# Seven-product FFN chunks that add up in PSUM, and gate chunk 2 in that form too

## The chip, the cores and the metric

The kernel runs on one core of a Trainium2 chip. The metric is the device time in microseconds of one execution; three executions are given, and one more was profiled.

## What is computed

A decoder trunk of two layers on one sequence of 512 tokens with 1024 features, in fp32. Each layer is: half a SwiGLU FFN, a mixer (gated linear attention in the first layer, stick-breaking attention in the second), half a SwiGLU FFN. So there are four FFNs, and they are where the change is:

```python
def rmsnorm(x, g):
    return x * rsqrt(mean(x * x, axis=-1) + EPS) * g

def swiglu(h, w_gate, w_up, w_down):      # D_FF = 2816
    return (silu(h @ w_gate) * (h @ w_up)) @ w_down

x = x + 0.5 * swiglu(rmsnorm(x, ffn_norm), w_gate, w_up, w_down)
```

## The kernel before

Activations lie with features on the 128 partitions and the 512 tokens along the free axis. A product that must keep fp32 accuracy is made of three matmuls on rounded operands: a value is cut in a high part (ScalarE, ACT: a cast) and a low part (VectorE, DVE: value minus high part), and high x high, low x high and high x low are added up in PSUM. Names ending in h and l are these parts (wh, wl of weights; nh, nl of the normed input; hh, hl of a result that goes into the down projection).

**The queue.** All weight work is a list of entries in `feed.q`. Each entry has units (a weight chunk and a view of it) and a body with its matmuls. `Feed.start` (called as each entry begins) first splits the weights of this entry and the next two (at most four buffers of 1024 columns, tag wh and wl), then loads the raw chunks of six entries (two raw buffers of 1 MB), then runs the body. The framework puts the instructions on the engines' queues; among those that are ready the earlier in the program goes first.

**An FFN.** The 2816 gate and up columns are 11 chunks of 256 columns, c = 0 to 10. A plain chunk is two entries of `feat`, each 24 matmuls of 512 columns (8 blocks of features in, three matmuls each) into one tile ps_f. In the order of the queue, counted from the FFN's start: e0 to e3 are gate and up of chunk 0, e4 to e7 those of chunk 1, e8 and e9 gate of chunk 2; then come the chunks of `seven` (gate from chunk 3 on by `SEVEN`, up from chunk 2 on by `SEVEN_UP`), with entries of the down projection of the group before (`down`, 24 matmuls of 512 columns) put between them.

**Seven products.** `seven` computes a chunk as a 2 x 2 block product (features in by features out, with the tokens in two halves of H = 256) with seven block products in place of eight (Winograd's form of Strassen's scheme). Each product is 12 matmuls of 256 columns (4 blocks, three matmuls each). A chunk is two entries: `body_1` has four products (P1 to P4 in the prediction), `body_2` has three (P5 to P7). `body_1` uses the view ax of the raw weights and the weight sums s12, `body_2` uses the sums s34 and the view a22. The sums (`sums_12`, `sums_34`) are four DVE operations of 512 columns into tiles of tag s, and are made when the entry is split. On the input side the products use nh, nl and the eight input sums th, tl (`t_half`): t sums 0, 2, 4, 6 in `body_1`, and 1, 3, 5, 7 in `body_2`. Before the change, P1 to P7 end in these tiles and operations: w (copied to u2 by ACT, L545), z (added to u2 by DVE), q (copied to c5 by ACT, L552), w again (then Silu or the product with the gate), z's other half (u3 = z + u2, o1 = u3 + c5, on DVE), q again (o0 = q + u2, on DVE), w's other half (o1 = w + u3, on DVE).

**Start of an FFN.** `run` lets e0 and e1 run on input that isn't normed yet, while the statistics and their row R are made (`stats_a`, `stats_b`). Before each of e2 to e5, one piece of `normed_input` runs: two blocks scaled (xn, L592), split (nh, nl), and four differences for one tile ts (L608) of tag s, so that after four pieces the four buffers of tag s hold ts. Then `sums` makes the eight input sums, each half a ts tile: a cast th on ACT and a subtraction tl on DVE (both L598 and L599), in pieces 0 to 7, two before each of e6 to e9. A buffer of tag s is free again when both halves of its ts are split, and the weight sums s12 and s34 use the same four buffers.

Of the kernel before, what the change touches and what calls it, by code (L numbers as in the profile page):

```python
# [18 lines left out]
P = 128  # L19
T = 512  # L20
# [12 lines left out]
def decoder(ctx: ExitStack, tc: tile.TileContext, a: dict, out: bass.AP):  # L33
# [13 lines left out]
    def psum(name, tag=None):  # L47
        if tag is None:
            tag = order[turn_[0] % 8]
            turn_[0] += 1  # L50
        return pp.tile([P, T], F32, tag=tag, bufs=banks[tag], name=name)
# [11 lines left out]
    def mm(ps, l, r, first, last):  # L63
        nc.tensor.matmul(ps, l, r, start=first, stop=last)  # L64
# [27 lines left out]
    class Entry:  # L92
# [3 lines left out]

        def __init__(self, units, body, place=0, lead=False):
            self.units, self.body, self.W, self.place = units, body, None, place
            self.lead = lead

        def split(self):
            if self.W is None:
                self.W = []
                for ch, view, n, m in self.units:
                    r = view(ch.load())
                    few = n * m < 1024
                    if few:

                        h = st["few"].tile([P, n * m + NEAR], F32R, tag="vh", bufs=1, name="wh")[:, NEAR:]
                        l = st["few"].tile([P, n * m + 64 - NEAR], F32R, tag="vl", bufs=1, name="wl")[:, : n * m]  # L110
                    else:
                        h, l = (
                            wp.tile([P, n * m + 64], F32R, tag="w" + t, bufs=4, name="w" + t)[
                                :, self.place : self.place + n * m
                            ]
                            for t in "hl"
                        )
                    h, l = (t.rearrange("p (n m) -> p n m", m=m) for t in (h, l))
                    st["cut"] = nc.scalar.copy(h, r).ins  # L119
                    with tc.issue_after(st["gains"]):  # L120
                        nc.vector.tensor_tensor(out=l, in0=r, in1=h.bitcast(F32), op=ALU.subtract)  # L121
                    self.W.append((h, l))
                    if self.lead and len(self.W) == 1:

                        first = wp.tile([P, m], F32R, tag="w1", bufs=1, name="w1")
                        nc.scalar.copy(first, r[:, 0])
                        self.first = first

    class Feed:
# [3 lines left out]
        def start(self):  # L133
            i = self.pos
            self.pos += 1
            used = 0
            for e in self.q[i : i + 3]:
                used += sum(n * m >= 1024 for _, _, n, m in e.units)
                if used > 4:
                    break  # L140
                e.split()
            for e in self.q[i : i + 6]:
                for u in e.units:
                    u[0].load()
            e = self.q[i]
            return e.body(e.W)
# [234 lines left out]
    def stats_b(tag=None):  # L381

        ps = psum("ps_R", tag)
        dgs = sp.tile([P, T], F32, tag="ss", name="dg")
        for i in range(NT):
            dg = dgs[:, i * P : (i + 1) * P]
            nc.vector.tensor_scalar(
                out=dg, in0=ident, scalar1=st["r4"][:, i : i + 1], scalar2=None, op0=ALU.mult
            )
            mm(ps[:, i * P : (i + 1) * P], ones, dg, True, True)  # L390
        st["R"] = sp.tile([P, T], F32, tag="sq", name="R")
        nc.vector.tensor_copy(st["R"], ps)

# [28 lines left out]
    class FFN:  # L422
# [4 lines left out]


        GROUPS = ((0, 2), (2, 4), (4, 6), (6, 8), (8, 9), (9, 11))
        NORMED, SEVEN = 6, 3  # L430
        SEVEN_UP = (2, 3, 4, 5, 6, 7, 8, 9, 10)

        def __init__(self, wg, wu, wd, gi, nxt, first=False, last=False):
# [49 lines left out]
        def seven(self, ch, group=None):  # L483
# [30 lines left out]
            def half(k0, c):  # L514
                return lambda j: (st["h"][k0 + j][:, c * H : c * H + H], st["l"][k0 + j][:, c * H : c * H + H])

            def part(name):
                return self.tp.tile([P, H], F32, tag="c", bufs=2, name=name)

            def add(o, x, y):  # L520
                nc.vector.tensor_tensor(out=o, in0=x, in1=y, op=ALU.add)

            def left(o, w):
                if group is None:
                    nc.scalar.activation(o[:, 0:H], w, AF.Silu)
                else:
                    nc.vector.tensor_tensor(out=o[:, 0:H], in0=w, in1=self.gates[0][:, 0:H], op=ALU.mult)

            def rest(o, c):
                if group is None:  # L530
                    st["silu"] = nc.scalar.activation(o[:, c:T], o[:, c:T], AF.Silu).ins
                    self.gates.append(o)
                    return
                nc.vector.tensor_tensor(out=o[:, c:T], in0=o[:, c:T], in1=self.gates.pop(0)[:, c:T], op=ALU.mult)
                self.close(o, group)

            def body_1(W):
                ax, s = W

                v["w"], v["z"], v["q"] = psum("ps_w"), psum("ps_z"), psum("ps_q")  # L540
                w, z, q = (v[n][:, 0:H] for n in "wzq")
                v["o"] = self.tp.tile([P, T], F32, tag="t", name="o0")
                prod(w, ax, 0, half(0, 0), lead=entry.first if lead else None)
                v["u2"] = part("u2")
                nc.scalar.copy(v["u2"], w)  # L545
                yield
                prod(z, s, 4, lambda j: self.t_half(1, j))
                add(v["u2"], z, v["u2"])
                yield
                prod(q, s, 0, lambda j: self.t_half(0, j))  # L550
                v["c5"] = part("c5")
                nc.scalar.copy(v["c5"], q)  # L552
                yield
                prod(w, ax, 4, half(4, 0), first=False)
                left(v["o"], w)
                yield

            def body_2(W):
                s, a22 = W
                q, y = v["q"][:, 0:H], v["z"][:, H:T]  # L560
                o0, o1 = v["o"], self.tp.tile([P, T], F32, tag="t", name="o1")
                prod(y, s, 0, lambda j: self.t_half(2, j))
                u3 = o1[:, 0:H]
                add(u3, y, v["u2"])
                nc.vector.tensor_tensor(out=o1[:, H:T], in0=u3, in1=v["c5"], op=ALU.add)
                yield
                prod(q, s, 4, half(4, 1), first=False)
                add(o0[:, H:T], q, v["u2"])
                rest(o0, H)
                yield  # L570
                o = v["w"][:, H:T]
                prod(o, a22, 0, lambda j: self.t_half(3, j))
                add(o1[:, 0:H], o, u3)
                rest(o1, 0)
                yield


# [47 lines left out]
        def sums(self):  # L625
            def piece(i):

                h = np_.tile([P, T], F32R, tag="xh", name="th")
                l = np_.tile([P, T], F32R, tag="xl", name="tl")
                self.ts[i] = self.cut(h, l, self.ts[i].rearrange("p a b -> p (a b)"))  # L630

            return [lambda i=i: piece(i) for i in range(KD)]

        def evac_g(self, ps):
            t = self.tp.tile([P, T], F32, tag="t", name="t")
# [17 lines left out]
        def run(self, between=None):  # L653
            with tc.tile_pool(name="hp", bufs=8, reuse_waits="tile") as self.hp, tc.tile_pool(
                name="tp", bufs=5, reuse_waits="tile"
            ) as self.tp:
                st["few"] = self.hp
                new_norm()
                two_halves(stats_a)
                stats_b()  # L660
                flush(self.defer)
                for job, n in ((self.normed_input, self.NORMED - 2), (self.sums, self.sums_by - self.NORMED)):
                    todo = list(job())
                    for i in range(n):
                        for piece in todo[i * len(todo) // n : (i + 1) * len(todo) // n]:
                            piece()
                        feed.entries(1)
                    self.normed = True
                    st["h"], st["l"] = zip(*self.n)
                feed.entries(self.count - self.sums_by)  # L670
                if between is not None:
                    with tc.issue_after(st["silu"]):
                        nc.scalar.preload_act_table_set("sqrt_and_others")
                    feed.q[feed.pos].split()
                    between(self.tp)
                feed.entries(self.total - self.count)
# [636 lines left out]
```

## Time and profile before

| | us |
|---|---|
| three executions | 1870.85, 1871.63, 1871.76 |
| median | 1871.63 |
| the profiled execution | 1871.49 |
| its span on the core | 1869.6 |
| TensorE (PE) busy | 1849.7 (99%) |
| DVE busy | 1456.8 (78%) |
| ACT busy | 954.0 (51%) |

Busy times are those of the profiled execution, and the shares are of its span. PE is the matmul stream and PEld its weight loads, which overlap it. In the rows of the profile, L64 are the matmuls of the plain entries and of the down entries, L510 those of the seven-product chunks, L119 and L121 the casts and subtractions that split weights, L493 to L500 the weight sums, L598 and L599 the split of inputs and results, and L297 the addition of a down product to x. The mean of a matmul in a row is longer than the distance from one to the next, since matmuls overlap; the distance is what counts.

### The profile page before, as it was taken

Reading aid. Unit: us, or ns where it says so; the run is one execution under the profiler, and the core shown is the slowest. Engines: PE = TensorE matmul, PEld = TensorE weight load, DVE = VectorE, ACT = ScalarE, POOL = GpSimd, SP = SyncE. Lnnn points to the kernel's source line nnn. Section 1 sums busy time; section 2 is a strip of 40 time slices with the busy share of each in tenths; the row PEclk is TensorE's granted clock in tenths of the full one; section 3 lists DMA queues with packets and bytes.
Section 4 is the critical chain, followed back from the end, with each engine's and each line's share of the span. In section 5 each row is a group of like instructions: output and inputs, shape, how many; then the busy total and the mean of one; then the engine's idle time right before and its main releaser. Section 6 shows DMA issues by size and latency. Waiting matters only on the chain.

```text
span 1869.6 us, 28889 instructions
## 1 busy us (share of the span) xinstructions
PE 1849.7 (99%) x11789; PEld 1647.6 (88%) x11789; DVE 1456.8 (78%) x2313; ACT 954.0 (51%) x1506; POOL 7.3 (0%) x17
## 2 busy tenths in 40 slices
PE   8999999999999999999999999999999999999998
PEld 6899999789887899999888999998888788999997
DVE  7978777775766988877888778776878769778785
ACT  6534434444555544444554444445888755444444
POOL 0000000100000000000000000000000000000000
PEclk9999999999999999999999999999999999999999
DMA  5423333212223233342233333233221223333321
GB/s 158 146 91 112 103 113 105 86 50 65 64 72 113 77 104 103 108 129 80 79 113 124 102 102 113 79 93 100 68 68 57 68 91 95 120 102 102 119 85 68
DMA packets 177514, 179.03 MB, mean 96 GB/s; under 512 B 4035, under 2 KB 167925, under 8 KB 177381
## 3 DMA queue, kind: packets, MB, share of 16 engines
q1 hardware_dynamic: 176768, 176.18, 30.1%
q8 instruction: 92, 1.51, 0.3%
q0 software_dynamic: 512, 0.99, 0.2%
q14 instruction: 42, 0.34, 0.1%
q10 hardware_dynamic: 100, 0.03, 0.0%
HBM read 175.11 MB, written 2.10 MB: 95 GB/s over the span
## 4 chain that ended last, share of the span: by engine, by line
PE 96%; DVE 2%; ACT 1%; DMA 1%; issue 0%; DVEq 0%; ACTq 0%; SPq 0%
PE ps_d L64 25%; PE ps_f L64 20%; PE ps_w L510 15%; PE ps_z L510 10%; PE ps_q L510 10%; PE ps_t L64 5%; PE ps_b L64 4%; PE ps_S L64 1%; PE ps_z L1044 1%; PE ps_bt L64 1%; PE ps_oT L1106 1%; PE ps_T L1091 1%; PE ps_o L64 1%; DVE wl L121 0%; DMA raw<-in_ffn_w_up_dram 0%; PE ps_R L64 0%
## 5 line engine op out<-in xcount | busy, mean ns | idle before, releaser
L121 DVE TENSOR_TENSOR wl<-raw,wh 128x1024 fp32r<-128x1024 f32 x244 | 261.3, 1071 | 81.8 <-ACT wh L119 71.6
L119 ACT CAST wh<-raw 128x1024 fp32r<-128x1024 f32 x244 | 226.5, 932 | 137.4 <-PE ps_f L64 44.3
L64 PE MATMUL ps_d<-hh,wl 128*128 128x512 f32 x672 | 262.1, 390 | 0.0
L64 PE MATMUL ps_d<-hh,wh 128*128 128x512 f32 x672 | 262.1, 390 | 0.0
L64 PE MATMUL ps_d<-hl,wh 128*128 128x512 f32 x672 | 261.4, 389 | 0.0
L119 ACT CAST wh<-s 128x1024 fp32r<-128x1024 f32 x136 | 142.8, 1050 | 142.4 <-PE ps_q L510 70.4
L297 DVE SCALAR_TENSOR_TENSOR x<-ps_d,x 128x512 f32<-128x512 f32 x184 | 125.6, 688 | 87.6 <-PE ps_d L64 87.4
L121 DVE TENSOR_TENSOR wl<-s,wh 128x1024 fp32r<-128x1024 f32 x136 | 166.2, 1222 | 25.9 <-ACT wh L119 15.3
L64 PE MATMUL ps_f<-xh,wh 128*128 128x512 f32 x448 | 181.7, 406 | 3.1 <-DVE q L707 1.5
L64 PE MATMUL ps_f<-xl,wh 128*128 128x512 f32 x448 | 175.0, 391 | 0.0
L64 PE MATMUL ps_f<-xh,wl 128*128 128x512 f32 x448 | 174.5, 389 | 0.0
L119 ACT CAST wh<-rawd 128x1024 fp32r<-128x1024 f32 x84 | 88.5, 1054 | 150.7 <-PE ps_d L64 127.6
L510 PE MATMUL ps_z<-th,wh 128*128 128x256 f32 x544 | 150.3, 276 | 0.0
L510 PE MATMUL ps_z<-th,wl 128*128 128x256 f32 x544 | 150.2, 276 | 0.0
L510 PE MATMUL ps_z<-tl,wh 128*128 128x256 f32 x544 | 150.1, 276 | 0.0
L510 PE MATMUL ps_w<-nh,wl 128*128 128x256 f32 x544 | 150.1, 276 | 0.0
L510 PE MATMUL ps_w<-nl,wh 128*128 128x256 f32 x544 | 150.1, 276 | 0.0
L64 PEld LDWEIGHTS ps_d<-hl,wh 128*128 128x128 f32 x672 | 126.2, 188 | 26.7
L64 PEld LDWEIGHTS ps_d<-hh,wh 128*128 128x128 f32 x672 | 126.2, 188 | 24.8
L64 PEld LDWEIGHTS ps_d<-hh,wl 128*128 128x128 f32 x672 | 126.1, 188 | 24.1
L121 DVE TENSOR_TENSOR wl<-rawd,wh 128x1024 fp32r<-128x1024 f32 x84 | 102.9, 1225 | 42.8 <-ACT wh L119 33.6
L510 PE MATMUL ps_w<-nh,wh 128*128 128x256 f32 x488 | 134.7, 276 | 0.0
(249 smaller groups left out, 4711.7 us busy)
## 6 DMA issues: line engine op xcount, KB each, us to landing
raw<-in_ffn_w_gate_dram SPq DMA_DIRECT2D x43, 1024.0 KB, 5.4
raw<-in_ffn_w_up_dram SPq DMA_DIRECT2D x43, 1024.0 KB, 5.3
rawd<-in_ffn_w_down_dram SPq DMA_DIRECT2D x84, 512.0 KB, 3.5
raw<-in_gla_w_in_dram SPq DMA_DIRECT2D x12, 1024.0 KB, 5.3
raw<-in_sb_w_in_dram SPq DMA_DIRECT2D x16, 512.0 KB, 3.8
raw<-in_gla_w_out_dram SPq DMA_DIRECT2D x4, 1024.0 KB, 5.1
raw<-in_sb_w_in_dram SPq DMA_DIRECT2D x4, 1024.0 KB, 5.1
raw<-in_sb_w_out_dram SPq DMA_DIRECT2D x4, 1024.0 KB, 5.0
```

The costliest lines, as they stand in the source:

```text
L64: nc.tensor.matmul(ps, l, r, start=first, stop=last)
L119: st["cut"] = nc.scalar.copy(h, r).ins
L121: nc.vector.tensor_tensor(out=l, in0=r, in1=h.bitcast(F32), op=ALU.subtract)
L297: nc.vector.scalar_tensor_tensor(out=xs[k], in0=ps, scalar=0.5, in1=xs[k], op0=ALU.mult, op1=ALU.add)
L510: nc.tensor.matmul(o, l_, r_, start=first and j + n == 0, stop=j == 3 and n == 2, skip_group_check=True)
L1044: nc.tensor.matmul(o_, l_, r_, start=first, stop=last, skip_group_check=True)
L1091: nc.tensor.transpose(ps[:, c0 : c0 + P], ys[yb][:, yc + j * P : yc + (j + 1) * P], ident)
L1106: nc.tensor.matmul(po[e * 64 : e * 64 + 64, j * P : T], self.v[j][:, c : c + 64], self.wt[p, e][bk][:, c0 : c0 + n], start=j == 0, stop=j ...
```

## The change

It has five parts. (1) `SEVEN` is 2 in place of 3, so that the gate columns of chunk 2 are also made in seven products: e8 and e9 are then `body_1` and `body_2` of that chunk, and one down entry follows each chunk of this group. (2) In the bodies, three products go on adding in w (P1, P3, P5, P7, with copies of the sums in between), and z begins as an ACT copy of w after P1, onto which P4 adds. ACT copies q into o1, w into o0 and w into u3. Three DVE additions and the tiles u2 and c5 go. The Silu, or the product with the gate, is made in four parts of 256 columns by `gate`. (3) `Feed.start` also makes the views, and so the weight sums, of one entry more than it splits (`view`). (4) The input sums are made in the order 0, 1, 2, 4, 6, then `body_1` of the first seven-product chunk, then 3, 5, 7; the first five stand before e6 and e7. (5) The four matmuls of `stats_b` that spread R are one accumulation group of the bank.

```diff
         def split(self):
-                for ch, view, n, m in self.units:
-                    r = view(ch.load())
+                for r, (_, _, n, m) in zip(self.view(), self.units):
...
                 e.split()
+            for e in self.q[i : i + 4]:
+                e.view()
...
-            mm(ps[:, i * P : (i + 1) * P], ones, dg, True, True)
+            nc.tensor.matmul(
+                ps[:, i * P : (i + 1) * P], ones, dg, start=i == 0, stop=i == NT - 1, skip_group_check=True
+            )
...
-        NORMED, SEVEN = 6, 3
+        NORMED, SEVEN = 6, 2
...
+            def gate(o, c, t):
+                if group is None:
+                    st["silu"] = nc.scalar.activation(o[:, c : c + H], t, AF.Silu).ins
                 else:
+                    g = self.gates[0 if o is v["o"][0] else 1]
+                    nc.vector.tensor_tensor(out=o[:, c : c + H], in0=t, in1=g[:, c : c + H], op=ALU.mult)
             def body_1(W):
                 ax, s = W
...
                 prod(w, ax, 0, half(0, 0), lead=entry.first if lead else None)
-                v["u2"] = part("u2")
-                nc.scalar.copy(v["u2"], w)
-                yield
-                prod(z, s, 4, lambda j: self.t_half(1, j))
-                add(v["u2"], z, v["u2"])
+                nc.scalar.copy(z, w)
                 yield
                 prod(q, s, 0, lambda j: self.t_half(0, j))
-                v["c5"] = part("c5")
-                nc.scalar.copy(v["c5"], q)
-                yield
-                prod(w, ax, 4, half(4, 0), first=False)
-                left(v["o"], w)
+                nc.scalar.copy(o1[:, H:T], q)
+                yield
+                prod(w, s, 4, lambda j: self.t_half(1, j), first=False)
+                nc.scalar.copy(o0[:, H:T], w)
+                yield
+                prod(z, ax, 4, half(4, 0), first=False)
+                gate(o0, 0, z)
                 yield
             def body_2(W):
                 s, a22 = W
...
-                prod(y, s, 0, lambda j: self.t_half(2, j))
-                u3 = o1[:, 0:H]
-                add(u3, y, v["u2"])
-                nc.vector.tensor_tensor(out=o1[:, H:T], in0=u3, in1=v["c5"], op=ALU.add)
+                prod(w, s, 0, lambda j: self.t_half(2, j), first=False)
+                u3 = self.tp.tile([P, H], F32, tag="c", bufs=1, name="u3")
+                nc.scalar.copy(u3, w)
+                nc.vector.tensor_tensor(out=o1[:, H:T], in0=u3, in1=o1[:, H:T], op=ALU.add)
                 yield
                 prod(q, s, 4, half(4, 1), first=False)
-                add(o0[:, H:T], q, v["u2"])
-                rest(o0, H)
-                yield
-                o = v["w"][:, H:T]
-                prod(o, a22, 0, lambda j: self.t_half(3, j))
-                add(o1[:, 0:H], o, u3)
-                rest(o1, 0)
+                nc.vector.tensor_tensor(out=o0[:, H:T], in0=q, in1=o0[:, H:T], op=ALU.add)
+                gate(o0, H, o0[:, H:T])
+                if group is not None:
+                    self.close(o0, group)
+                gate(o1, H, o1[:, H:T])
+                yield
+                prod(w, a22, 0, lambda j: self.t_half(3, j), first=False)
+                gate(o1, 0, w)
...
-            return [lambda i=i: piece(i) for i in range(KD)]
+            return [lambda i=i: piece(i) for i in (0, 1, 2, 4, 6, 3, 5, 7)]
...
-                for job, n in ((self.normed_input, self.NORMED - 2), (self.sums, self.sums_by - self.NORMED)):
...
+                spread(self.normed_input(), self.NORMED - 2)
+                self.normed = True
+                st["h"], st["l"] = zip(*self.n)
+                todo = self.sums()
+                spread(todo[:5], self.sums_by - self.NORMED)
+                feed.entries(1)
+                for piece in todo[5:]:
+                    piece()
+                feed.entries(self.count - self.sums_by - 1)
```

More of the change, by code (lines that the diff above doesn't have):

```diff
@@ L98, in __init__, with view @@
             self.units, self.body, self.W, self.place = units, body, None, place
-            self.lead = lead
+            self.lead, self.views = lead, None
+        def view(self):
+            if self.views is None:
+                self.views = [view(ch.load()) for ch, view, _, _ in self.units]
+            return self.views
         def split(self):
@@ L515, in half @@
                 return lambda j: (st["h"][k0 + j][:, c * H : c * H + H], st["l"][k0 + j][:, c * H : c * H + H])
[L517 to L523, printed above, removed]
+            def gate(o, c, t):
                 if group is None:
-                    nc.scalar.activation(o[:, 0:H], w, AF.Silu)
+                    st["silu"] = nc.scalar.activation(o[:, c : c + H], t, AF.Silu).ins
@@ L526, in left @@
                 else:
[L527 to L535, printed above, removed]
+                    g = self.gates[0 if o is v["o"][0] else 1]
@@ L537, in body_1 @@
+                    nc.vector.tensor_tensor(out=o[:, c : c + H], in0=t, in1=g[:, c : c + H], op=ALU.mult)
             def body_1(W):
                 ax, s = W
-                v["w"], v["z"], v["q"] = psum("ps_w"), psum("ps_z"), psum("ps_q")
-                w, z, q = (v[n][:, 0:H] for n in "wzq")
-                v["o"] = self.tp.tile([P, T], F32, tag="t", name="o0")
+                v["w"], v["q"] = psum("ps_w"), psum("ps_q")
+                z = psum("ps_z")[:, 0:H]
+                w, q = (v[n][:, 0:H] for n in "wq")
@@ L543, in body_1 @@
+                o0, o1 = v["o"] = [self.tp.tile([P, T], F32, tag="t", name=n) for n in ("o0", "o1")]
                 prod(w, ax, 0, half(0, 0), lead=entry.first if lead else None)
-                v["u2"] = part("u2")
-                nc.scalar.copy(v["u2"], w)
-                yield
-                prod(z, s, 4, lambda j: self.t_half(1, j))
-                add(v["u2"], z, v["u2"])
+                nc.scalar.copy(z, w)
                 yield
                 prod(q, s, 0, lambda j: self.t_half(0, j))
-                v["c5"] = part("c5")
@@ L559, in body_2 @@
                 s, a22 = W
-                q, y = v["q"][:, 0:H], v["z"][:, H:T]
-                o0, o1 = v["o"], self.tp.tile([P, T], F32, tag="t", name="o1")
-                prod(y, s, 0, lambda j: self.t_half(2, j))
-                u3 = o1[:, 0:H]
-                add(u3, y, v["u2"])
-                nc.vector.tensor_tensor(out=o1[:, H:T], in0=u3, in1=v["c5"], op=ALU.add)
+                w, q = (v[n][:, 0:H] for n in "wq")
+                o0, o1 = v["o"]
+                prod(w, s, 0, lambda j: self.t_half(2, j), first=False)
+                u3 = self.tp.tile([P, H], F32, tag="c", bufs=1, name="u3")
+                nc.scalar.copy(u3, w)
+                nc.vector.tensor_tensor(out=o1[:, H:T], in0=u3, in1=o1[:, H:T], op=ALU.add)
                 yield
                 prod(q, s, 4, half(4, 1), first=False)
-                add(o0[:, H:T], q, v["u2"])
-                rest(o0, H)
-                yield
-                o = v["w"][:, H:T]
-                prod(o, a22, 0, lambda j: self.t_half(3, j))
-                add(o1[:, 0:H], o, u3)
-                rest(o1, 0)
+                nc.vector.tensor_tensor(out=o0[:, H:T], in0=q, in1=o0[:, H:T], op=ALU.add)
[3 more added lines that the diff above has]
+                gate(o1, H, o1[:, H:T])
+                yield
+                prod(w, a22, 0, lambda j: self.t_half(3, j), first=False)
+                gate(o1, 0, w)
+                if group is not None:
+                    self.close(o1, group)
+                    del self.gates[:2]
+                else:
+                    self.gates += [o0, o1]
                 yield
@@ L661, in run, with spread @@
                 flush(self.defer)
-                for job, n in ((self.normed_input, self.NORMED - 2), (self.sums, self.sums_by - self.NORMED)):
-                    todo = list(job())
+                def spread(todo, n):
                     for i in range(n):
@@ L667, in run @@
                         feed.entries(1)
-                    self.normed = True
-                    st["h"], st["l"] = zip(*self.n)
-                feed.entries(self.count - self.sums_by)
+                spread(self.normed_input(), self.NORMED - 2)
[7 more added lines that the diff above has]
+                feed.entries(self.count - self.sums_by - 1)
                 if between is not None:
```

## The prediction

> **What bounds the kernel now.** I read the page first (shares, then the chain that ended last), then the chain in order of time, then the busy time by stretch of the first feed-forward stage, then the queues of VectorE (DVE) and ScalarE (ACT) there.
>
> ```profile
> span 1869.6 us, 28889 instructions
> PE 1849.7 (99%) x11789; PEld 1647.6 (88%) x11789; DVE 1456.8 (78%) x2313; ACT 954.0 (51%) x1506; POOL 7.3 (0%) x17
> PE 96%; DVE 2%; ACT 1%; DMA 1%; issue 0%; DVEq 0%; ACTq 0%; SPq 0%
> ```
>
> TensorE (PE) carries 96% of the chain. The chain by pieces shows how tightly: start, length, engine and tile.
>
> ```profile
> 27.75 43.56 PE ps_f L64 x192
> 610.60 43.56 PE ps_f L64 x192
> 948.95 43.56 PE ps_f L64 x192
> 1532.80 43.56 PE ps_f L64 x192
> ...
> 71.31 1.36 PE ps_w L510 x12
> ...
> 124.40 1.36 PE ps_q L510 x12
> ...
> 127.12 1.36 PE ps_z L510 x12
> ```
>
> The four FFN stages open alike: eight plain entries (e2 to e9) of 24 matmuls of 512 columns each, 192 in 43.56 us, so 226.9 ns a matmul and 5.445 us an entry, without a gap; then seven-product chunks, 12 matmuls of 256 columns in 1.36 us, 113.3 ns each. So a product P1 to P7 is 1.36 us. PE has no slack to give back here except fewer matmul columns.
>
> The second fact is DVE. Columns: stretch, its length, then busy time (and count) of PE, PEld, DVE, ACT, POOL, granted clock, DMA share, GB/s.
>
> ```profile
> 28.00:49.00 21.00, 21.00 (x94) 17.33 (x94) 21.00 (x39) 13.61 (x20) 0.00 (x0) 1.00 0.04 10
> 49.00:71.00 22.00, 22.00 (x99) 18.22 (x98) 21.95 (x34) 10.53 (x16) 0.00 (x0) 1.00 0.48 151
> 71.00:90.00 19.00, 19.00 (x169) 18.96 (x168) 16.21 (x26) 11.22 (x17) 0.00 (x0) 1.00 0.43 137
> ...
> 120.00:353.00 233.00, 233.00 (x1616) 215.64 (x1615) 185.21 (x279) 106.29 (x161) 2.43 (x3) 1.00 0.33 105
> ```
>
> From 28 to 71 us DVE is busy 42.95 of 43 us; later it is at 79% (185.21 of 233). At the opening two engines are full at once, and the chunk that changes its form lies exactly there.
>
> **Part 1: gate chunk 2 in seven products.** It removes e8 and e9 (48 matmuls x 226.9 ns = 10.89 us) and adds 84 matmuls x 113.3 ns = 9.52 us. Gain 1.37 us per FFN, 5.5 us for four, as long as PE stays without gaps. The Trainium skill (TensorE: Matmul & The Clock Gate, "Wait — 56ns, not 53.3ns?") adds a fixed 2.5 ns per matmul to N divided by 2.4 GHz, which speaks against halving the columns; by it 48 x 215.8 − 84 x 109.2 gives 1.19 us, an estimate, 4.7 us in all. The rows show no such term (113.3 is half of 226.9), so 5.5 stands. The granted clock is 1.00 in every stretch above and nothing here lowers it.
>
> **Part 2: the bodies of the 68 (now 72) chunks.** Three DVE additions of 256 columns go (u2, u3, the last o1), two ACT copies come, and a 512-column product or Silu becomes two of 256.
>
> ```profile
> L521 DVE TENSOR_TENSOR u<-ps_z,u 128x256 f32<-128x256 f32 x68 | 28.6, 420 | 12.5 <-PE ps_z L510 12.5
> L545 ACT COPY u<-ps_w 128x256 f32<-128x256 f32 x68 | 25.3, 372 | 10.7 <-PE ps_w L510 7.6
> ```
>
> DVE loses about 3 x 0.42 us of busy time a chunk, ACT gains 2 x 0.37. Neither is on the chain in the steady part, so it is worth nothing there by itself. What is new is what PE waits for: P3 (into w) for the copy z<-w, P5 (into w) for o0<-w, P7 for u3<-w. Each copy has one product, 1.36 us, to get done. The steady part shows ACT at these points:
>
> ```profile
> 121.76 1.06 ACT L119 CAST wh<-rawd 128x1024 fp32r<-128x1024 f32 x1 [1.64 <-PE ps_d L64]
> 122.72 0.29 ACT L126 CAST w<-raw 128x128 fp32r<-128x128 f32 x1
> 123.08 0.37 ACT L545 COPY u<-ps_w 128x256 f32<-128x256 f32 x1
> 125.86 0.37 ACT L552 COPY c<-ps_q 128x256 f32<-128x256 f32 x1 [2.40 <-PE ps_q L510]
> 126.12 1.05 ACT L119 CAST wh<-raw 128x1024 fp32r<-128x1024 f32 x1
> ```
>
> The third product ends at 125.76 (124.40 + 1.36), the copy then runs to 126.23, and the fifth begins at 127.12: 0.9 us to spare, and the weight cast that could be in its way comes after it in the queue. I take 0 for the steady part. If the cast went first (1.05 + 0.37 us against 1.36, with 0.1 us to start) PE would lose about 0.2 us.
>
> **Part 3: the first chunk's operands, where the price lies.** e8 now needs at 60.4 us (71.31 − 2 x 5.445) what was needed at 71.3: split weights of ax and s12 by P2 (61.8), the t sums 0, 2, 4, 6, and by P5 (65.9) the split of s34 and the t sums 1, 3, 5, 7. These are DVE's rows (wl: split of weights, hl: of a result, tl: of a t sum, s: weight sums):
>
> ```profile
> 53.32 0.68 DVE L599 TENSOR_TENSOR tl<-ts,th 128x512 fp32r<-128x512 f32 x1
> 53.92 0.68 DVE L645 TENSOR_TENSOR t<-t 128x512 f32<-128x512 f32 x1
> 54.52 0.69 DVE L599 TENSOR_TENSOR tl<-ts,th 128x512 fp32r<-128x512 f32 x1
> 55.12 1.22 DVE L121 TENSOR_TENSOR wl<-raw,wh 128x1024 fp32r<-128x1024 f32 x1
> 56.26 0.69 DVE L599 TENSOR_TENSOR hl<-t,hh 128x512 fp32r<-128x512 f32 x1
> 56.86 1.29 DVE L599 TENSOR_TENSOR tl<-ts,th 128x512 fp32r<-128x512 f32 x2
> 58.06 1.22 DVE L121 TENSOR_TENSOR wl<-raw,wh 128x1024 fp32r<-128x1024 f32 x1
> ...
> 60.54 0.69 DVE L645 TENSOR_TENSOR t<-ps_f,t 128x512 f32<-128x512 f32 x1
> 61.15 1.22 DVE L121 TENSOR_TENSOR wl<-raw,wh 128x1024 fp32r<-128x1024 f32 x1
> 62.28 0.68 DVE L599 TENSOR_TENSOR hl<-t,hh 128x512 fp32r<-128x512 f32 x1
> 62.88 0.69 DVE L493 TENSOR_TENSOR s<-raw 128x512 f32<-128x512 f32 x1
> ...
> 64.08 0.68 DVE L494 TENSOR_TENSOR s<-s,raw 128x512 f32<-128x512 f32 x1
> ```
>
> From start to start a 1024-column split takes 1.14 us (55.12 to 56.26), a 512-column operation 0.60. The order follows the program among what is ready. Two things hold it: the chunk's raw weights and the buffers of tag s.
>
> ```profile
> 52.14 2.00 ACT L119 CAST wh<-raw 128x1024 fp32r<-128x1024 f32 x2
> ...
> 64.86 1.05 ACT L119 CAST wh<-s 128x1024 fp32r<-128x1024 f32 x1 [2.97 <-DVE s L494]
> ```
>
> The raw gate chunk 2 is cast from 52.14, so nothing of it is ready earlier. And all four s buffers hold ts; s12 gets one when t sums 0 and 1 are split (55.12), s34 the next when 2 and 3 are. I lay DVE's queue from 55.12, before which nothing differs: ax split to 56.26; first s12 sum 56.86; hl of e5 57.46; second s12 sum 58.06 (its cast on ACT, 1.05, to 59.2); tl 2 and 4 to 59.26; s12 split 60.40; tl 6 61.00; a22 split 61.60; L645 of e7 62.20; tl 3 62.80; tl 5 63.40; s34 sums 64.60; cast on ACT to 65.75, meanwhile hl of e7 and an s12 sum of the next chunk to 65.80; s34 split 66.94; split for the down entry 68.08; second s12 sum of the next chunk 68.68; tl 7 69.28. So P1 to P4 are served. P5 starts at 65.9 and stands from its second matmul until 66.94, about 1.0 us; then tl 7, wanted 1.0 us into P5 at about 67.9, comes at 69.3: 1.4 us more. Loss 2.4 us per FFN against the gain of 1.37: +1.03, for four +4.1 us. ACT's own copy before P5 falls into the same wait.
>
> Bounds of this term: 0 if the four operations that can wait (hl e5, L645, hl e7, down split: 0.60 x 3 + 1.14 = 2.94 us) stand behind s34 and tl 7, which is more than the 2.4; 3.4 if the down entry's cast gets its buffer at e7's end and its split (1.14) comes ahead of tl 3, so that s34's ends at 68.1 and, with tl 7 and next-chunk sums (0.60 each) also ahead, 69.3. I take 2.4, since program order among ready operations is what the rows show.
>
> Behind it DVE recovers: a chunk and a down entry give it 9.52 + 5.45 us of PE time, at 79% load. One-entry-earlier weight sums, the extra early-weight copies (0.29 each on ACT) and the flags of the R matmuls change no count on the chain: nothing. The earlier view of an entry issues no new load, since every start already loads six entries ahead; what it can hold up is DVE's queue, where its sums stand ahead of the body's operations, and that is in the layout above.
>
> **Sum.** The profiled execution took 1871.49 us (span 1869.6 and 1.9 around), 0.14 below the median of 1871.63. 1871.6 − 5.5 + 4 x 2.4 = 1875.7 us. Its own range, 2.0 to 2.9 us lost per FFN: 1874.1 to 1877.7.
>
> **Rivals.** (A) The queue keeps up, and P5 is not late: 1871.6 − 5.5 = 1866.1; it counts as faster below a loss of 0.43 us per FFN, that is if s34's split is done by about 66.3 and tl 7 by about 68. For it: the 2.94 us of work that can wait, and the t sums put in the order 0, 1, 2, 4, 6. Against: 42.95 of 43 us busy, and sums 3, 5, 7 placed behind e8. Chance 0.20. (B) It half keeps up, for instance tl 7 ahead of the down split, a loss of 0.43 to 2.0: 1867.8 to 1874.1. Chance 0.20. (C) The down split first, a loss of 2.9 to 3.5: 1877.7 to 1880.1. Chance 0.20. (D) ACT's copies in the bodies: a cast ahead of one copy per chunk costs 0.2 us x 72 = 14 us, with part 3 1866.1 + 14 + 9.6 = 1890, alone 1880. It decides from any cast that starts within the product before. Against: the copy at 125.86 stands ahead of the cast. Chance 0.06. The Trainium skill (PSUM — Partial Sum Buffer, "PSUM bank collisions raise a hardware error") says the chip doesn't arbitrate two engines on one bank, so these waits cannot be loosened; no row here shows a collision.
>
> **How the numbers follow.** The forecast has 0.34, A to C 0.20 each, D 0.06. About 0.2% (3.7 us) is what a measurement of this kernel can tell from no change. Slower by more needs over 1875.4, a loss above 2.3: C, D and two thirds of the forecast, 0.20 + 0.06 + 0.22 = 0.48. Same: B and the rest, 0.32. Faster: A, 0.20. The range goes from A (1866.0) to C's end (1880.0); it leaves out D and tails.
>
> **What would show it.** Right: after the six plain entries PE idles 2 to 3 us at the first P5 of each FFN (around 66, and at the same place of the other three), released by DVE wl and tl, with no gap elsewhere; DVE's busy time falls, ACT's rises; of the plain ps_f matmuls 192 go and 336 of line 510's kind come. Wrong: no gap there (A); gaps of 0.2 us with ACT copies as releasers in many chunks (D); a gap at P1 or P2 already, which would mean that the s12 chain, not s34's, is late.

## The result and the profile after

| | us |
|---|---|
| before, nine executions | median 1872.02 (1870.85 to 1872.92) |
| after, nine executions | median 1877.15 (1876.42 to 1877.94) |
| ratio | 1.0027, 95% interval 1.0017 to 1.0037 |
| profiled execution of after | 1877.22, span 1875.1 |

The changed kernel is slower by 5.1 us. The forecast was 1875.7 in a range of 1866.0 to 1880.0, so sign and range hold. The account behind the number holds only in part, as the experiments show: the first chunk costs half of what was forecast, and the other half of the loss lies where the prediction wrote 0.

From the page of the changed kernel: span, busy time of the engines with their instructions, and the chain that ended last by engine.

```profile
span 1875.1 us, 29147 instructions
PE 1853.9 (99%) x11933; PEld 1655.6 (88%) x11933; DVE 1411.2 (75%) x2177; ACT 1012.4 (54%) x1714; POOL 7.3 (0%) x17
PE 94%; DVE 2%; ACT 2%; DMA 1%; issue 1%; DVEq 0%; ACTq 0%; SPq 0%
```

DVE lost 45.6 us of busy time (1456.8 before), ACT gained 58.4 (954.0), PE has 144 matmuls more (4 x (84 - 48)). PE is busy 4.2 us *more*, though its columns are worth 5.5 us less. The page alone can't say why.

The chain of the changed kernel by pieces (start, length, engine and tile), the openings of the four FFNs:

```profile
27.75 32.66 PE ps_f L64 x144
611.06 32.68 PE ps_f L64 x144
950.58 32.68 PE ps_f L64 x144
1536.67 32.68 PE ps_f L64 x144
```

The six plain entries cost what was forecast (144 x 226.8 ns). Where the time goes shows in the pieces behind them, here of the first FFN:

```profile
60.41 1.48 PE ps_w L520 x13
61.89 1.41 PE ps_q L520 x12
...
85.70 1.41 PE ps_w L520 x12
87.11 5.24 PE ps_d L64 x23
92.35 1.36 PE ps_w L520 x12
93.71 0.33 PE ps_d L64
94.04 1.37 PE ps_q L520 x12
95.41 1.36 PE ps_w L520 x12
```

(The chain's starts lie some 0.16 us behind those of the timeline, which the next fences show. Line numbers shift with the edits: L520 here is L510 of before, L124 and L126 are L119 and L121, L603 is L599.) There are three things that no row of before has:

- **A wait at the first P5** of each FFN, around 66 us in the first.
- **Lone matmuls.** `ps_d x1` stands between P1 and P2: the first matmul of the down entry that follows the chunk was put there, and takes 0.33 us in place of 0.227. `x13` in the first line is the same thing: the thirteenth is the first matmul of the next chunk.
- **A slower pitch.** From 61.89 to 87 most products take 1.41 us, later ones 1.36. A matmul of 256 columns then starts 118 ns (117.8 in the mean) after the one before instead of 113, at a granted clock that reads 1.00 in both stretches.

To weigh them, I summed over the four FFNs what exceeds 113.3 ns (256 columns) or 226.7 ns (512) from the start of each matmul to the next, in each kernel's profile. In us, with the kernels of the experiments below:

| kernel | wait and moved matmuls, first two chunks | behind lone matmuls, later | pitch of 118 | all, with short ones | median |
|---|---|---|---|---|---|
| before | 0 | 0 | 0.0 | 1.7 | 1872.0 |
| after | 4.6 | 2.9 | 2.9 | 13.7 | 1877.2 |
| e1 q first | 4.3 | 0.4 | 2.4 | 9.9 | 1873.6 |
| e2 / e12 bodies only | 0 | 2.2 / 2.2 | 1.1 / 4.1 | 5.6 / 8.6 | 1877.6 / 1877.8 |
| e3 chunk 2 only | 3.7 | 0 | 1.7 | 7.6 | 1870.7 |
| e4 q first, down between | 0 | 0.4 | 2.8 | 6.0 | 1869.0 |
| e5 old bodies, down between | 0 | 0 | 2.1 | 4.3 | 1867.1 |
| e6 down between | 0 | 2.3 | 1.7 | 6.9 | 1872.4 |
| e7 bodies, q first | 0 | 0.6 | 1.5 | 4.2 | 1873.7 |
| e8 as e5, with a lead | 0 | 0 | 0.0 | 2.2 | 1865.1 |
| e9 as e4, with a lead | 0 | 0.4 | 0.0 | 3.2 | 1866.5 |
| e10 before, no lead | 0 | 0 | 25.4 | 26.9 | 1896.2 |

After against before is 13.7 - 1.7 = 12.0 us lost against 5.5 gained, +6.5; the spans differ by 5.5. What is left, about 1 us here and up to 2 us in the other rows, lies outside these stretches of the FFNs, and I have not followed it.

**The first P5.** The timeline of the changed kernel there, DVE and PE:

```profile
65.79 0.68 DVE L603 TENSOR_TENSOR tl<-ts,th 128x512 fp32r<-128x512 f32 x1
65.85 0.28 PE L520 MATMUL ps_z<-nl,wh 128*128 128x256 f32 x1
...
66.12 0.39 PE L520 MATMUL ps_w<-th,wh 128*128 128x256 f32 x1
...
66.35 0.28 PE L520 MATMUL ps_q<-nh,wh 128*128 128x256 f32 x1
66.39 1.22 DVE L126 TENSOR_TENSOR wl<-s,wh 128x1024 fp32r<-128x1024 f32 x1
...
67.07 0.73 PE L64 MATMUL ps_d<-hh,wh 128*128 128x512 f32 x2 [0.44 <-ACT wh L124]
...
67.66 0.39 PE L520 MATMUL ps_w<-th,wl 128*128 128x256 f32 x1
```

P4's last matmul starts at 65.85, so P5 is due at 65.97. Its first matmul starts at 66.12, when the cast of s34 on ACT has ended (66.07). The split of s34 (`wl<-s`) ends at 67.61 (66.39 + 1.22), and P5's second matmul starts at 67.66. The last t sum (`tl`, 65.79) stands ahead of the split and is no second wait. In between PE did what had been put into its queue at that place: one matmul of P5, one of P6 and two of the down entry, 2 x 0.113 + 2 x 0.227 = 0.68 of the 1.69 us. So about 1.0 us per FFN is lost, 1.15 with the smaller gaps around.

**A later chunk.** The timeline around the lone matmul at 93.55, PE, its weight loads (PEld) and ACT:

```profile
92.43 1.06 ACT L124 CAST wh<-rawd 128x1024 fp32r<-128x1024 f32 x1 [2.75 <-PE ps_d L64]
...
93.44 0.28 PE L520 MATMUL ps_w<-nl,wh 128*128 128x256 f32 x1
...
93.54 0.19 PEld L64 LDWEIGHTS ps_d<-hh,wh 128*128 128x128 f32 x1
93.55 0.49 PE L64 MATMUL ps_d<-hh,wh 128*128 128x512 f32 x1
93.65 0.19 PEld L520 LDWEIGHTS ps_q<-th,wh 128*128 128x128 f32 x1
...
93.88 0.28 PE L520 MATMUL ps_q<-th,wh 128*128 128x256 f32 x1
```

The lone matmul needs the cast of the down weights, which ends at 93.49. A weight load otherwise starts with the matmul ahead of its own, which would be 93.44; this one could start only at 93.54, and P2 comes at 93.88 instead of 93.78 (93.55 + 0.227). P2 had its operands and stood all the same. Of the 35 lone matmuls 28 have such a gap, and in each of the 28 the cast ended 0.05 to 0.07 us before the lone matmul started. The other 7 take 0.23 us and cost nothing; there the cast had ended 1.35 us before or more (at 294.58 for instance). The Trainium skill (TensorE: Matmul & The Clock Gate, "The mechanism") states that matmuls start and end strictly in program order; these rows agree, since a ready P2 waited 0.1 us for a matmul that belonged to a later entry.

### The profile page after: what moved, and what is told of

The parts are those of the page before. It is cut to its first block, busy times and chain, and to the rows that moved or that the text cites. A ratio compares the mean times of both kernels' runs of the same rounds, so it can differ in the third digit from the quotient of the medians.

```text
span 1875.1 us, 29147 instructions
## 1 busy us (share of the span) xinstructions
PE 1853.9 (99%) x11933; PEld 1655.6 (88%) x11933; DVE 1411.2 (75%) x2177; ACT 1012.4 (54%) x1714; POOL 7.3 (0%) x17
## 4 chain that ended last, share of the span: by engine, by line
PE 94%; DVE 2%; ACT 2%; DMA 1%; issue 1%; DVEq 0%; ACTq 0%; SPq 0%
PE ps_d L64 25%; PE ps_w L520 21%; PE ps_f L64 17%; PE ps_q L520 10%; PE ps_z L520 5%; PE ps_t L64 5%; PE ps_b L64 4%; PE ps_S L64 1%; PE ps_bt L64 1%; PE ps_z L1055 1%; PE ps_oT L1117 1%; PE ps_T L1102 1%; PE ps_o L64 1%; ACT wh L124 1%; DVE wl L126 0%
## 5 line engine op out<-in xcount | busy, mean ns | idle before, releaser
L126 DVE TENSOR_TENSOR wl<-raw,wh 128x1024 fp32r<-128x1024 f32 x244 | 259.2, 1063 | 101.3 <-ACT wh L124 57.2
L124 ACT CAST wh<-raw 128x1024 fp32r<-128x1024 f32 x244 | 224.8, 923 | 130.0 <-PE ps_f L64 44.2
L520 PE MATMUL ps_w<-th,wh 128*128 128x256 f32 x864 | 239.6, 277 | 0.0
L520 PE MATMUL ps_w<-th,wl 128*128 128x256 f32 x864 | 239.4, 277 | 0.0
L520 PE MATMUL ps_w<-tl,wh 128*128 128x256 f32 x864 | 239.2, 277 | 0.0
L126 DVE TENSOR_TENSOR wl<-s,wh 128x1024 fp32r<-128x1024 f32 x144 | 175.8, 1221 | 41.9 <-ACT wh L124 22.4
L124 ACT CAST wh<-s 128x1024 fp32r<-128x1024 f32 x144 | 151.2, 1050 | 94.1 <-PE ps_q L520 40.9
L124 ACT CAST wh<-rawd 128x1024 fp32r<-128x1024 f32 x84 | 88.5, 1054 | 194.1 <-issue 97.7
L520 PEld LDWEIGHTS ps_w<-th,wl 128*128 128x128 f32 x864 | 162.5, 188 | 0.9 <-DVE wl L126 0.8
L520 PEld LDWEIGHTS ps_w<-th,wh 128*128 128x128 f32 x864 | 162.2, 188 | 1.0 <-ACT wh L124 0.8
L520 PEld LDWEIGHTS ps_w<-tl,wh 128*128 128x128 f32 x864 | 162.2, 188 | 0.0
L64 PEld LDWEIGHTS ps_d<-hl,wh 128*128 128x128 f32 x672 | 126.2, 188 | 25.4
L126 DVE TENSOR_TENSOR wl<-rawd,wh 128x1024 fp32r<-128x1024 f32 x84 | 102.8, 1224 | 53.5 <-ACT wh L124 40.9
```

The source lines that it names most:

```text
L520: nc.tensor.matmul(o, l_, r_, start=first and j + n == 0, stop=j == 3 and n == 2, skip_group_check=True)
```

## Experiments

The order of TensorE's queue is fixed when the program is built, by the framework's own estimate of what will be ready, so the count of lone matmuls of a kernel is known before it runs: none in before, 35 single ps_d in after. Two theories stood against each other. Theory 1: the loss is matmuls out of order, with the slower pitch, and a smaller wait in the first chunk. Theory 2, the prediction's: the loss is all in the first chunk's DVE queue.

**e2: the new bodies alone, on the kernel before.** Its edit is the hunk of the change from `part` to `body_2`.

> The kernel before with the new bodies alone; gate chunk 2 stays plain. 26 single ps_d matmuls stand between P1 and P2 in the queue's order. Theory 1: 26 x 0.10 = 2.6, so 1872.0 + 2.6 = 1874.6 us. Theory 2: 1872.0 us, since DVE and ACT have time to spare there. A third case, casts ahead of the new ACT copies in many chunks (0.2 us each): above 1880 us.

Measured: 1877.6 us (1875.4 to 1879.0), ratio 1.0030 (1.0019 to 1.0042). So the bodies that I costed at nothing are slower than before by as much as the whole change (the two intervals overlap), with chunk 2 still plain. 26 lone matmuls stand in it, 22 of them with a gap. Yet theory 1's figure, 1874.6, is missed by 3 us: the lone matmuls have a second effect.

**e12: the same kernel again,** for its spread.

> The same kernel as e2_bodies_only, another profile and more times, since its runs spread from 1875.4 to 1879.0 us. If the spread comes from the pitch behind a lone matmul (each leaves the rest of its chunk at 113 or at 118 ns, 0.34 us): this profile's time differs from the other (span 1873.5 us) by as many 0.34 us as the count of chunks at 118 ns differs (3 there). Rival: the time differs and the count does not.

Measured: 1877.8 us (1876.1 to 1879.1); this profile's span is 1877.3, where e2's is 1873.5. The chain of e2 and, below it, of e12 at the same chunk:

```profile
262.09 1.36 PE ps_w L510 x12
263.45 0.33 PE ps_d L64
263.77 1.37 PE ps_q L510 x12
265.14 1.36 PE ps_w L510 x12
```

```profile
262.54 1.36 PE ps_w L510 x12
263.90 0.33 PE ps_d L64
264.23 1.41 PE ps_q L510 x12
265.64 1.41 PE ps_w L510 x12
```

One program, one place, and behind the lone matmul the chunk runs at 1.36 in one execution and at 1.41 in the other, to its end. e2's profile has 263 matmuls at 118 ns, e12's 918: 1.1 against 4.1 us. These 3.0 of the 3.8 us between the two spans are the pitch; 0.8 is not accounted for. So a lone matmul with a gap costs 0.1 us for certain and, in some executions, 72 x 4.45 ns = 0.32 us more.

**e1 and e7: bank q taken before bank w,** in the changed kernel and in the new bodies alone:

```diff
-                v["w"], v["q"] = psum("ps_w"), psum("ps_q")
+                v["q"] = psum("ps_q")
+                v["w"] = psum("ps_w")
```

> The changed kernel with one line altered: bank q is taken before bank w. In the order of TensorE's queue the single ps_d matmuls between P1 and P2 fall from 35 to 4; the first chunk stays as it is. Theory 1 (a matmul out of its place costs 0.10 us each, 28 of them with a gap): 1877.2 - 2.8 = 1874.4 us, and the gaps ahead of ps_q after a lone ps_d are gone. Theory 2 (the prediction's: the loss is all in the first chunk's DVE queue, the bodies cost nothing): 1877.2 us.

> The kernel before with the new bodies, bank q taken before bank w; gate chunk 2 stays plain. 6 lone ps_d matmuls instead of 26. Theory 1 (the bodies cost what the lone matmuls cost): 1872.0 + 0.6 = 1872.6 us. Rival (the bodies cost by their own waits, as the 1877.6 us of e2_bodies_only would leave room for): 1874 us or more.

Measured: e1 1873.6 us, against before 1.0011 (1.0002 to 1.0020); e7 1873.7 us, 1.0011 (1.0003 to 1.0020). The order of two allocations brings 3.5 and 3.9 us: the kernel's `psum` hands out the banks in turn, so the order decides which PSUM bank P2 goes to, and with the other bank the framework puts nothing between P1 and P2 in all but a few chunks. That its estimate finds the one bank free earlier than the other is my reading and not shown. e1 lies below theory 1's 1874.4. e7's two theories stood at 1872.6 and from 1874; it came out between, and its profile has 0.6 us behind the six lone matmuls left and 1.5 us of pitch, most of it where a lone matmul or a moved first matmul stands ahead. So by their own waits the bodies cost next to nothing: e2, e12 and e7 each have one gap of 0.3 us at a P3, in the last FFN (1826 to 1831 us), where a table load of 1.28 us on ACT stands ahead of the copy z<-w. But they don't give what they save on DVE either.

**e3: gate chunk 2 alone, in the kernel before** (`SEVEN = 2`, nothing else).

> The kernel before with gate chunk 2 in seven products and nothing else; no lone ps_d matmul in the later chunks. Theory 1: -5.5 us for the columns, back 1.1 us of wait and up to 0.65 us of slower matmuls in the first two chunks of each FFN: 1870.9 to 1873.5 us. Theory 2: the first chunk alone brings the whole loss of 2.9 us per FFN: 1872.0 - 5.5 + 11.6 = 1878.1 us.

Measured: 1870.7 us, 0.9996 (0.9987 to 1.0005). That is no difference from before that these runs can tell. Theory 1 (1870.9 to 1873.5) is closer than theory 2 (1878.1): by the table, part 1's gain of 5.5 us is there and is all but paid away, by 3.7 us at the first chunk and 1.7 us of pitch.

**e6 and e4: the first down entry between the halves of gate chunk 2,** so that P5's operands are wanted 5.4 us later; e6 is the changed kernel with this alone, e4 has bank q first too.

```diff
                             self.seven(g)
+                            if c == self.SEVEN:
+                                late = feed.q.pop()
+                                down(*downs[put])
+                                put += 1
+                                feed.q.append(late)
```

> The changed kernel with one thing altered: the first down entry between the two halves of gate chunk 2. The wait at P5 and the matmuls moved about there go (about 1.3 us per FFN, 5.4 us), the lone matmuls of the later chunks stay (39), the slower pitch stays. Theory 1: 1877.2 - 5.4 = 1871.8 us. Theory 2 (the first chunk is the whole loss): 1866.5 us.

> The changed kernel with bank q taken before w, and with the first down entry of each FFN put between the two halves of gate chunk 2, so that s34 and the last t sum are wanted 5.4 us later. In the queue's order nothing is left out of place in the first chunk, and 8 lone ps_d matmuls in the later ones. Theory 1: wait, slower matmuls and gaps all go: 1872.0 - 5.5 + 0.8 = 1867.3 us. Theory 2: 1866.5 us. Rival: the down entry's own weights are late at 65.9 us, and the wait moves there: 1 us or more per FFN, 1870.5 us or above.

Measured: e6 1872.4 us, 1.0004 (0.9995 to 1.0013), close to theory 1's 1871.8 and not theory 2's 1866.5; e4 1869.0 us, 0.9984 (0.9976 to 0.9993). No wait is left at the first P5 in either. e4 missed its 1867.3 by the pitch, 2.8 us, which I had expected to go with the moved matmuls. It didn't: most of it begins at P5, behind the down entry, with no matmul out of place near.

**e5 and e8: the old bodies in that frame, without and with a lead.** e5 is the kernel before with `SEVEN = 2`, the t sums in the new order and the down entry between. A chunk behind plain or down entries begins with a *lead* matmul, whose weights are a separate copy (tile w1) of the first block; the second half of gate chunk 2 now also follows a down entry, but has none. e8 gives it one:

```diff
                                 late = feed.q.pop()
+                                late.lead = True
...
-                prod(y, s, 0, lambda j: self.t_half(2, j))
+                prod(y, s, 0, lambda j: self.t_half(2, j), lead=second.first if second.lead else None)
```

> The kernel before with its old bodies, gate chunk 2 in seven products, the t sums in the new order, and the first down entry of each FFN between the two halves of gate chunk 2. No matmul stands out of its place in TensorE's queue. Theory 1 (wait, order and the slower pitch of 118 ns are the whole loss): 1872.0 - 5.5 = 1866.5, plus 0.5 to 0.7 us per FFN for the slower pitch from the fifth product of gate chunk 2 to the end of up chunk 2: 1868.5 to 1869.3 us. Theory 2 (a seven-product chunk 2 costs DVE and ACT time that comes back later, wherever the chunk stands): 1871 us or more.

> As e5_old_bodies_down_between, and the second half of gate chunk 2 begins, like a chunk behind plain or down entries, with a matmul whose weights are a small separate copy (the lead). Theory 1 (a run of 256-column matmuls that follows 512-column ones without a lead goes at 118 ns, with one at 113): 2.4 us under e5, 1866.5 us, and no product above 114 ns in the first two chunks. Rival (the pitch has to do with the place in the stage, or with what DVE does then): as e5, the products still at 118 ns.

Measured: e5 1867.1 us, 0.9976 (0.9967 to 0.9985); e8 1865.1 us, 0.9964 (0.9952 to 0.9977), the fastest of all. The chain of e5, then of e8, at the same place:

```profile
64.46 1.36 PE ps_w L515 x12
65.82 5.46 PE ps_d L64 x24
71.28 1.42 PE ps_z L515 x12
72.70 1.41 PE ps_q L515 x12
...
84.01 1.41 PE ps_w L515 x12
85.42 5.47 PE ps_d L64 x24
90.89 1.36 PE ps_w L515 x12
```

```profile
64.04 1.36 PE ps_w L516 x12
65.41 5.46 PE ps_d L64 x24
70.87 1.36 PE ps_z L516 x12
72.23 1.36 PE ps_q L516 x12
...
83.11 1.36 PE ps_w L516 x12
```

One matmul decides the pitch of the 120 behind it in each FFN: in e5 the ten products after the down entry take 1.41, and the next chunk, which has a lead, 1.36; in e8 all take 1.36.

**e10 and e11: the lead itself, on the kernel before** (two executions each). e10 sets `lead = False` everywhere. e11 keeps the leads and moves the copy by 64 bytes (`NEAR` is 16 numbers of 4 bytes):

```diff
-                        first = wp.tile([P, m], F32R, tag="w1", bufs=1, name="w1")
+                        first = wp.tile([P, m + 32], F32R, tag="w1", bufs=1, name="w1")[:, NEAR : NEAR + m]
```

> The kernel before without any lead: the first matmul of each chunk takes its weights from the full cast as the others do. If a run of 256-column matmuls without a lead goes at 118 ns: 68 chunks x 84 matmuls x 4.7 ns = 27 us slower, 1899 us. If the lead only serves to start early and the pitch comes from elsewhere: 1872.0 us, or a few us more where P1 then waits for the 1024-column cast, with products at 113 ns.

> The kernel before with its leads, but the lead's copy lies 64 bytes further, so that its address has the same remainder by 128 bytes as the other weights of the chunk (32) instead of that of the moving operands and of the plain weights (96). If the lead keeps the 113 ns pitch by its address: products at 118 ns as without a lead, 1896 us. If it does so by being a separate or an earlier copy: 1871.5 us, products at 113 ns.

Measured: e10 1896.2 us, 1.0131 (1.0112 to 1.0149); e11 1904.5 us, 1.0175 (1.0156 to 1.0193). The chain of e10:

```profile
99.89 7.25 PE ps_d L64 x32
107.15 1.42 PE ps_w L510 x12
108.56 1.41 PE ps_z L510 x12
```

and of e11:

```profile
27.81 44.17 PE ps_f L64 x192
71.98 1.41 PE ps_w L510 x12
73.40 1.37 PE ps_z L510 x12
74.77 1.36 PE ps_q L510 x12
76.12 1.41 PE ps_w L510 x12
77.54 1.37 PE ps_z L510 x12
78.91 1.41 PE ps_q L510 x12
...
108.21 1.41 PE ps_w L510 x12
109.62 1.41 PE ps_z L510 x12
```

Without leads every chunk runs at 118 ns: 68 x 84 x 4.45 = 25.4 us, against 24.9 measured.

e11 was to tell whether the lead's address does it, and it doesn't show that. By the addresses in the built program the moving operands, the plain weights and the lead start at 96 bytes past a multiple of 128, the other weights of the chunk at 32; in e11 the lead does too. But e11's wider tile also moved other tiles by 128 bytes: nh, nl, hh, hl, and the half-size weights that P7 reads. The time is lost where these are read. From the start of a matmul to the next, those of 512 columns take 233 ns on nh and nl and 232 on hh and hl (227 to 228 in before), and 227 on xl, which did not move. In 52 of the 68 chunks, the first one in the rows above among them, P1, P4, P6 and P7 read a moved tile and run at 118 ns, while P2, P3 and P5 read none and run at 113 to 114. Only the other 16 chunks run at 118 throughout, as every chunk of e10 does (the one at 108.21 is the first of them). So with the lead at remainder 32 the fast pitch is still there in most chunks. Of the 33 us about 12 lie in matmuls of 512 columns, which have no lead. What in the lead holds the pitch stays open: its place, its being a separate copy, or its being ready early.

**e9: the new bodies with all three mends** (q first, down between, lead).

> The new bodies with all three mends: bank q before w, the first down entry between the halves of gate chunk 2, and a lead for the second half. Theory 1 (bodies cost nothing but lone matmuls, of which 8 stand): the 1865.1 us of the old bodies in the same frame plus 0.1 to 0.45 us for each of 8: 1866 to 1869 us. Rival (the bodies gain by themselves, with 45 us less DVE work): under 1865 us.

Measured: 1866.5 us, 0.9972 (0.9961 to 0.9982), no matmuls at 118 ns to speak of. It isn't under e8. The new bodies bring nothing, though DVE has less to do.

## Why the prediction was right, and where it was not

**Part 1** (-5.5 us) holds: the openings take 32.7 in place of 43.6 us, and products at 1.36 are half of plain ones by the column. e8 shows it whole: with the losses gone, the kernel is 6.3 us under before, and in its profile the four FFNs take 5.4 us less. The fixed term per matmul of the Trainium skill, by which the gain would be 4.7, doesn't show in products at 113 ns. At 118 ns a matmul takes 4.45 ns more, but that comes and goes with the lead (e5 and e8, before and e10) and not with the count.

**Part 2** is the step that failed. It looked for waits of P3, P5 and P7 on ACT's copies, found 0.9 us to spare and wrote 0. Those waits did not come in the changed kernel: no gap of its later chunks stands at P3 or P5. But the bodies cost about 6 us by themselves (e2). About 4 of them come from a new order of allocations: it changed which bank P2 writes, and the framework put a matmul of a later entry ahead of P2 (e7 gives the 3.9 us back). In after, 2.9 us lie behind lone matmuls. I had asked whether a copy would be late on the chip, and not what order the queue would have. Rival D named the right place, steady chunks, and a price of 0.2 us each, with the wrong cause: what stood in the way was a matmul ahead of P2 and not a cast ahead of a copy.

**Part 3** was mis-sized, 2.4 us per FFN for 1.15. Its first half held: P5's first matmul starts, the second waits for the split of s34, "about 1.0 us". That the split was later (67.61, not 66.94) was made good by 0.68 us of other matmuls put there. Its second half, 1.4 us for t sum 7, did not happen: the row at 65.79 stands *before* the split. The layout took program order among ready operations; the queue is in the order of the framework's estimate, which had put the t sum first.

**The sum** came out near, 1875.7 for 1877.15, and that is luck, because two errors cancel: the 5.0 us too many of part 3 (4 x 1.25) stand against 5.8 us that no part had (2.9 behind lone matmuls, and 2.9 of pitch, most of it in the first two chunks: the lead of the second was moved into the first, so the second begins without it). The sign "slower" had 0.48 and is what happened; the reason given for it carries 4.6 of the 12.0 us lost.

**What would show it** asked for a gap of 2 to 3 us at the first P5 and none elsewhere. The gap is 1.0 to 1.15, and there are others: by the prediction's own test its account was wrong in the steady part.

Parts 3 to 5 of the change (the views one entry ahead, the order of the t sums, the statistics) were not run each by itself. e5 and e8 have the order of the t sums and not the views.

## What to carry to other kernels

Where a framework orders the queues by its own estimate, compare the order of the bottleneck engine's instructions before and after a change, not only their count: a lone instruction of a later stage inside a tight run is a wait taken early. When an edit "off the critical path" touches buffer allocation, its price is in that order, and one line (the order of two allocations, a down entry moved) can give it back. And an odd little copy in a tuned kernel may hold a pitch (taking the leads out of before costs 24.9 us): find what it keeps before putting a new kind of transition beside it.

## What the runs showed of the hardware

Matmuls of 256 columns have two steady pitches here, 113.3 and 118 ns, at a granted clock of 1.00 in both, and a run can keep its pitch for a hundred matmuls and more (the 120 of each FFN in e5). Behind matmuls of 512 columns and without a lead the pitch is 118 (all 68 chunks of e10, ten products of each FFN in e4 and e5), with a lead it is 113 (before, e8). Behind a gap of 0.1 us it is either, from one execution to the next (e2 and e12). Matmuls of 512 columns keep 226.7 ns in both. In e11, where tiles lie 128 bytes further, matmuls that read a moved tile are slower (233 for 227 ns, 118 for 113), and those of 512 columns that read none are not. What in the array or its reads holds this state stays open.
